# Weight remainders and mixer steps moved from GpSimd to VectorE in a two-block network on one core

## Chip, core and metric

The kernel runs on one core of a Trainium2 chip. The metric is the device time of one execution in microseconds (us), the median of three runs. A core has five engines that run side by side, each with its own queue that is worked off in order: TensorE (PE, with its weight loads shown as PEld), VectorE (DVE), ScalarE (ACT), GpSimd (POOL) and SyncE (SP), which here only issues loads. An instruction waits on semaphores at the head of its engine's queue; everything behind it on that engine waits too.

## What is computed

A sequence of 256 tokens of width 1024 goes through two different blocks, all in float32. The first has two layers of feed-forward, mixer, feed-forward; the second has a mixing stage (retention and dilated attention), a feed-forward and a gated embedding.

```
for layer in range(2):
    x = x + 0.5 * swiglu(rmsnorm(x, norm_ffn1[layer]), ffn1_gate, ffn1_up, ffn1_down)
    x = x + hybrid_mixer(rmsnorm(x, norm_mix[layer]), ...)      # three mixers side by side
    x = x + 0.5 * swiglu(rmsnorm(x, norm_ffn2[layer]), ffn2_gate, ffn2_up, ffn2_down)
x = rmsnorm(x, norm_final)
# second block
proj = rmsnorm_2(h, g_pre_mix) @ w_in_2
h = h + rmsnorm_2(mixed @ w_o_2, g_post_mix)       # mixed: retention and dilated attention, gated
h = h + rmsnorm_2(square(relu(rmsnorm_2(h, g_pre_mlp) @ w_up_2)) @ w_down_2, g_post_mlp)
h = h + rmsnorm_2(sigmoid(rmsnorm_2(h, g_pre_ple) @ w_ple_gate_2 + b) * (p @ w_ple_in_2), g_post_ple)
```

The hybrid mixer joins a gated delta rule (with a triangular solve over 128 tokens), a gated linear attention (scores by halving levels) and a gated linear recurrence.

## The kernel before

Weights stream from DRAM once, in 562 chunks of mostly 256 rows by 512 columns, loaded by SP into `raw` (four buffers). For accuracy each chunk is split into two tiles: `wh` is the chunk rounded by a ScalarE copy (L94), and `wl = raw - wh` is the remainder, one two-input subtraction (L97 on GpSimd, L99 on VectorE). `wh` and `wl` have three buffers each. A product then takes three matmuls for each weight tile and token tile: L146 to L148 where tokens are the output's rows (`gemm_tok`), L190 to L192 where features are (`gemm_feat`). The activations are split in the same way after a transpose on TensorE (`split`, L199 to L203).

Who computes a remainder is set by a string, `split_on`, read cyclically: "p" is GpSimd, "v" is VectorE. Outside the mixers it is "ppv", two of three on GpSimd. In a mixer each product has a string of its own in `MIX_ORDER`, which also is the order in which the mixer's steps are emitted: the recurrence's product `rg`, the small product `ba`, `k`, the decays (`gates`), the delta rule's keys and first solve (`dk`, `solve0`), the linear attention (`hg`, `vg`, `hgs`), and so on. `HG_POOL` says for each of the seven levels of `hgs` which engine computes the exponents (L900, L901) and the keys (L903). Four more steps of a mixer are fixed on GpSimd: the masks of the solve (L718, L719), the product of query and key (L871), and the gates of the recurrence (L988, L989, L995, L996).

The steps of VectorE in a mixer that the text names: the convolution of the recurrence (L964, L967) and of the delta rule (L628), the polynomial of a softplus (L383, L384), the predicated copies of the solve (L716), the queries of a level (L909). Every norm ends in a chain of tiny VectorE steps for x to the power -0.5 (L212 to L229).

The code is emitted in one order, and a scheduler then fixes each engine's queue ahead of the run, with priorities by that order and durations of its own. So a change of engine moves other instructions as well.

Of the kernel before, what the change touches and what calls it, by code (L numbers as in the profile page):

```python
# [19 lines left out]
# w ** -0.5 near 1 as a quadratic  # L20
# [3 lines left out]
class Weights:  # L24
    """All large weights as one array in DRAM, chunk after chunk in the order of use, each chunk
    with one contiguous run a partition. The host's side of it is laid out as chunks are taken."""
# [12 lines left out]
class Weight:  # L39
# [3 lines left out]
    def chunk(self, k0, nkt, c0, n):  # L43
        """Rows k0..k0+nkt*P, columns c0..c0+n as [P, nkt, n]."""
        a = self.all
        part = self.array[k0:k0 + nkt * P, c0:c0 + n].reshape(nkt, P, n).transpose(1, 0, 2)
        a.parts.append(part.reshape(-1))
        o, a.off = a.off, a.off + part.size
        return a.dram[o:a.off].rearrange("(p k c) -> p k c", p=P, k=nkt)


class Ctx:
    """Pools, constants and the pieces every sublayer uses."""

    def __init__(self, tc, stack):
# [15 lines left out]
        self.nw = 0  # L71
        self.nx = 0
        self.xtags = ("xa", "xb")   # two banks each; a phase may keep to one pair
        self.split_on = "ppv"   # who takes the remainders of the weight chunks: GpSimd or DVE
# [12 lines left out]
    def wchunk(self, w, k0, nkt, c0, n, room=None):  # L87
# [7 lines left out]
        self.nw += 1  # L95
        if self.split_on[self.nw % len(self.split_on)] == "p":
            nc.gpsimd.tensor_tensor(l, raw, h.bitcast(F32), op=ALU.subtract)  # L97
        else:
            nc.vector.tensor_tensor(l, raw, h.bitcast(F32), op=ALU.subtract)  # L99
# [14 lines left out]
    def hT_tile(self, j, dtype=None):  # L114
        """The j-th (h, l) pair of 8-k-tile slots."""
        return tuple(self.keep.tile([P, 8, S], F32R, tag=f"hT{i}{j}", name=self.nm("hT")) for i in "hl")

    def scratch(self, which):
        """A slot of a hidden-operand tile as 2048 plain floats a partition."""
# [6 lines left out]
    def gemm_tok(self, xs, w, kt0, nkt, c0, n, outs=None, first=True, last=True, wk0=0):  # L126
        """xs: (h, l) of [P, KT, S]; w: dram [K, N]; k-tiles kt0..kt0+nkt of xs, columns c0..c0+n."""
# [11 lines left out]
    def mm_tok(self, o, xs, kt0, m, t, wh, wl, a, z):  # L139
        """o += x[:, token tile t] @ w over m k-tiles from kt0, in three float32r products each."""  # L140
# [9 lines left out]
    def gemm_rows(self, xs, w, nkt, tail, js):  # L150
        """[P tok, 1024] for both token tiles as outs[ch][t]; the last tail weight chunks of each half
        are taken by token tile, so that tile 0 is ready before tile 1. js: hidden-operand slots that
        are free to hold them."""
# [52 lines left out]
    def rsqrt(self, out, x, shape, mul=None):  # L206
        """out = mul * x ** -0.5 for x > 0 (tiles of the given shape); mul: a number or a [P, 1] tile."""
# [24 lines left out]
class Stream:  # L232
    """The residual stream, token-major, and its transposed and weighted form for the next product."""
# [8 lines left out]
    def norm_T(self, wT, extra=None, by_tok=False):  # L242
        """(h, l): x * w transposed, split; r: [P, 2] rsqrt(mean(x^2) + eps)."""
# [45 lines left out]
def hidden_T(c, hT, hc, t, f0, n):  # L289
    """Transpose hc [P tok, n] into hT[:, f0/P.., t-th half], split."""  # L290
# [42 lines left out]
def consts_np():  # L333
    """Tables that depend on shapes alone: [P, n, P]."""
# [3 lines left out]
    out["triu"] = (t <= s) * 1.0            # [s', s]: s' <= s  # L338
    out["sufs"] = (t > s) * 1.0             # [s', s]: s' > s
    out["negm"] = np.where(t > s, -1e30, 0.0)   # [s, t]: s > t  # L340
    own = lambda a: np.stack([a[r, 32 * (r // 32):32 * (r // 32) + 32] for r in range(P)])   # diagonal 32-blocks
# [1171 lines left out]
```

## Time and profile before

| quantity | value |
|---|---|
| runs of the kernel | 1861.69 us median (1858.45, 1861.69, 1861.82) |
| the profiled execution, first to last instruction | 1858.6 us |
| TensorE busy | 1764.4 us, 95% |
| VectorE busy | 935.6 us, 50% |
| ScalarE busy | 896.4 us, 48% |
| GpSimd busy | 925.1 us, 50% |
| mean granted TensorE clock | 0.974 |

The first mixer lies at about 205 to 410 us and the second at about 786 to 1000 us; before, between and after them are the feed-forwards, and the second block begins at about 1180 us. In these tables "busy" of an engine is the time in which one of its instructions runs, also when that instruction is itself held up; so a long mean duration of a small operation is to be compared with the shortest one of its kind.

### The profile page before, as it was taken

To read this page: it belongs to the slowest core of one execution; us is meant where nothing else is said; L and a number is where in the kernel's file an instruction comes from. 1 tells how busy PE (TensorE), PEld (TensorE's weight loads), DVE (VectorE), ACT (ScalarE), POOL (GpSimd) and SP (SyncE) were. 2 spreads that over 40 slices of the span, in tenths; PEclk is the share of its full clock that TensorE was granted. 3 is DMA by queue.
4 is the path that set the end of the run, shared out by engine and by line. 5 is a ranking of instruction groups with operands and counts; after the bars stand their busy time and mean duration, and the time that the engine had idled before them with its cause. 6 is when DMAs were issued, how large, how long until landed. Compare 5 with 4: busy or idle time off the path is not lost.

```text
span 1858.6 us, 24550 instructions
## 1 busy us (share of the span) xinstructions
PE 1764.4 (95%) x9216; PEld 1488.6 (80%) x9216; DVE 935.6 (50%) x1744; ACT 896.4 (48%) x1364; POOL 925.1 (50%) x449
## 2 busy tenths in 40 slices
PE   8999988999999999987889999999999999999995
PEld 6888877978888788877878888788878888778884
DVE  5334599853333332299964333533556543643246
ACT  4445563444444444455345445455444544555453
POOL 4556455235555555544415556454433455555561
PEclk9999988899999999998989999999999999999998
DMA  6546432235555555532224545455333456545561
GB/s 221 181 159 206 162 111 74 87 102 181 182 193 182 181 182 181 182 137 91 69 100 169 177 163 205 153 184 173 127 134 114 158 176 209 181 164 181 182 227 45
DMA packets 91639, 292.13 MB, mean 157 GB/s; under 512 B 11008, under 2 KB 23808, under 8 KB 91520
## 3 DMA queue, kind: packets, MB, share of 16 engines
q1 hardware_dynamic: 91376, 290.45, 46.0%
q8 instruction: 72, 1.18, 0.3%
q14 instruction: 47, 0.39, 0.1%
q10 hardware_dynamic: 144, 0.11, 0.0%
HBM read 289.47 MB, written 1.05 MB: 156 GB/s over the span
## 4 chain that ended last, share of the span: by engine, by line
PE 72%; DVE 15%; issue 6%; POOL 3%; ACT 2%; DMA 1%; DVEq 0%; SPq 0%; POOLq 0%; ACTq 0%
PE mm L147 21%; PE mm L148 21%; PE mm L146 20%; POOL wl L97 3%; DVE cv L628 2%; PE htr L295 2%; PE mm L191 1%; PE mm L192 1%; PE mm L190 1%; DVE scr L909 1%; DMA raw<-in_weights 1%; DVE wl L99 1%; ACT wh L94 1%; DVE hS L716 1%; DVE rxc L967 1%
## 5 line engine op out<-in xcount | busy, mean ns | idle before, releaser
L97 POOL TENSOR_TENSOR wl<-raw,wh 128x1024 fp32r<-128x1024 f32 (+2 forms) x359 | 839.1, 2340 | 808.3 <-ACT wh L94 754.4
L94 ACT CAST wh<-raw 128x1024 fp32r<-128x1024 f32 (+2 forms) x544 | 549.5, 1011 | 600.7 <-PE mm L148 442.6
L147 PE MATMUL mm<-wl,xTh 128*128 128x512 f32 (+2 forms) x1336 | 509.0, 383 | 10.1 <-DVE wl L99 8.8
L148 PE MATMUL mm<-wh,xTl 128*128 128x512 f32 (+2 forms) x1336 | 503.9, 381 | 8.3 <-DVE xTl L203 8.3
L99 DVE TENSOR_TENSOR wl<-raw,wh 128x1024 fp32r<-128x1024 f32 (+2 forms) x185 | 236.4, 1278 | 488.3 <-ACT wh L94 487.9
L146 PE MATMUL mm<-wh,xTh 128*128 128x512 f32 (+2 forms) x1336 | 474.1, 385 | 1.4 <-ACT wh L94 0.9
L147 PEld LDWEIGHTS mm<-wl,xTh 128*128 128x128 f32 x1336 | 254.5, 190 | 58.6 <-DVE wl L99 9.3
L148 PEld LDWEIGHTS mm<-wh,xTl 128*128 128x128 f32 x1336 | 253.4, 190 | 59.5 <-DVE xTl L203 11.2
L146 PEld LDWEIGHTS mm<-wh,xTh 128*128 128x128 f32 x1336 | 250.7, 190 | 51.8 <-ACT xTh L202 3.2
L147 PE MATMUL mm<-wl,hT 128*128 128x512 f32 x608 | 243.3, 401 | 2.8 <-POOL wl L97 2.6
L148 PE MATMUL mm<-wh,hT 128*128 128x512 f32 x608 | 240.3, 396 | 0.0
L146 PE MATMUL mm<-wh,hT 128*128 128x512 f32 x608 | 219.1, 397 | 4.8 <-DVE scr L571 4.8
L190 PE MATMUL mm<-xTh,wh 128*128 128x256 f32 x448 | 130.7, 295 | 14.1 <-DVE xp L620 14.1
L146 PEld LDWEIGHTS mm<-wh,hT 128*128 128x128 f32 x608 | 115.3, 190 | 30.8 <-DVE scr L571 5.2
L147 PEld LDWEIGHTS mm<-wl,hT 128*128 128x128 f32 x608 | 115.8, 190 | 29.6 <-POOL wl L97 5.4
L148 PEld LDWEIGHTS mm<-wh,hT 128*128 128x128 f32 x608 | 116.1, 191 | 24.4 <-DVE hT L203 0.3
L191 PE MATMUL mm<-xTl,wh 128*128 128x256 f32 x448 | 131.9, 296 | 1.1 <-DVE xTl L203 1.1
L192 PE MATMUL mm<-xTh,wl 128*128 128x256 f32 x448 | 129.6, 294 | 0.0
L190 PEld LDWEIGHTS mm<-xTh,wh 128*128 128x128 f32 x448 | 88.5, 198 | 15.8 <-issue 15.5
L191 PEld LDWEIGHTS mm<-xTl,wh 128*128 128x128 f32 x448 | 89.0, 199 | 3.4 <-DVE xTl L203 1.9
L192 PEld LDWEIGHTS mm<-xTh,wl 128*128 128x128 f32 x448 | 87.6, 198 | 2.0 <-issue 1.2
L200 DVE TENSOR_TENSOR hT<-htr,hT 128x512 fp32r<-128x512 f32 (+1 forms) x76 | 49.9, 660 | 75.6 <-ACT hT L199 75.6
(444 smaller groups left out, 1857.6 us busy)
## 6 DMA issues: line engine op xcount, KB each, us to landing
raw<-in_weights SPq DMA_DIRECT2D x514, 512.0 KB, 3.3
raw<-in_weights SPq DMA_DIRECT2D x32, 256.0 KB, 3.1
raw<-in_weights SPq DMA_DIRECT2D x16, 260.0 KB, 3.0
x_res<-in_x SPq DMA_DIRECT2D x2, 512.0 KB, 4.4
rowp<-in_b_gate SPq DMA_DIRECT2D x2, 512.0 KB, 5.3
out<-pg SPq DMA_DIRECT2D x4, 256.0 KB, 2.0
tab<-in_tab SPq DMA_DIRECT2D x1, 900.5 KB, 6.0
ctab<-in_tab SPq DMA_DIRECT2D x1, 900.0 KB, 9.5
```

The lines of the kernel that those rows point to most:

```text
L94: nc.scalar.copy(h, raw)
L97: nc.gpsimd.tensor_tensor(l, raw, h.bitcast(F32), op=ALU.subtract)
L99: nc.vector.tensor_tensor(l, raw, h.bitcast(F32), op=ALU.subtract)
L146: nc.tensor.matmul(o, xh[:, kt, tok], wh[:, k], start=a and k == 0, stop=False)
L147: nc.tensor.matmul(o, xh[:, kt, tok], wl[:, k], start=False, stop=False)
L148: nc.tensor.matmul(o, xl[:, kt, tok], wh[:, k], start=False, stop=z and k == m - 1)
L190: nc.tensor.matmul(o, wh[:, k, cs], xh[:, kt], start=a, stop=False)
L191: nc.tensor.matmul(o, wh[:, k, cs], xl[:, kt], start=False, stop=False)
L192: nc.tensor.matmul(o, wl[:, k, cs], xh[:, kt], start=False, stop=z)
L200: nc.vector.tensor_tensor(l, src, h.bitcast(F32), op=ALU.subtract)
L295: nc.tensor.transpose(ps[:, b], hc[:, b * P:(b + 1) * P], c.ident)
L628: nc.vector.scalar_tensor_tensor(o[:, b], xp[:, b2, tap:tap + S], wc(tap), o[:, b], op0=ALU.mult, op1=ALU.add)
```

## The change

All `wl` subtractions go to VectorE, in every product. So do the solve's two masks, the query-key product, the exponents and keys of all levels, and the four steps of the recurrence. GpSimd keeps memsets and one-input copies. The strings that chose the engine go away; the order of emission stays. (The diff also drops comments, so line numbers of the kernel after are a little lower: L99 becomes L93, L967 becomes L955.)

```diff
-        self.nw += 1
-        if self.split_on[self.nw % len(self.split_on)] == "p":
-            nc.gpsimd.tensor_tensor(l, raw, h.bitcast(F32), op=ALU.subtract)
-        else:
-            nc.vector.tensor_tensor(l, raw, h.bitcast(F32), op=ALU.subtract)
+        nc.vector.tensor_tensor(l, raw, h.bitcast(F32), op=ALU.subtract)
...
-MIX_ORDER = "rg:pvvp ba:pvvp k:pvpp gates dk solve0 hg:vppv vg:pppv hgs v:ppvp solve1 hgo both dv1 q:ppvp dv0 dq core0 core1 z:ppvv dout out:pvvvppvp".split()
-HG_POOL = ("vvvppvp", "ppvppvv")
+MIX_ORDER = "rg ba k gates dk solve0 hg vg hgs v solve1 hgo both dv1 q dv0 dq core0 core1 z dout out".split()
...
-        nc.gpsimd.tensor_tensor(LT32, LT, h4(K["mt32"]), op=ALU.mult)
-        nc.gpsimd.tensor_tensor(LT, LT, h4(K["mt64"]), op=ALU.mult)
+        nc.vector.tensor_tensor(LT32, LT, h4(K["mt32"]), op=ALU.mult)
+        nc.vector.tensor_tensor(LT, LT, h4(K["mt64"]), op=ALU.mult)
...
-        nc.gpsimd.tensor_tensor(qk, q, k, op=ALU.mult)
+        nc.vector.tensor_tensor(qk, q, k, op=ALU.mult)
...
-            on = lambda i: nc.gpsimd if HG_POOL[i][lv] == "p" else nc.vector
-            on(0).tensor_tensor(Av[:, :, 1], cv[:, :, 1], ref, op=ALU.subtract)
-            on(0).tensor_tensor(Av[:, :, 0], ref, cv[:, :, 0], op=ALU.subtract)
+            nc.vector.tensor_tensor(Av[:, :, 1], cv[:, :, 1], ref, op=ALU.subtract)
+            nc.vector.tensor_tensor(Av[:, :, 0], ref, cv[:, :, 0], op=ALU.subtract)
...
-            on(1).tensor_tensor(B, A, k, op=ALU.mult)
+            nc.vector.tensor_tensor(B, A, k, op=ALU.mult)
...
-        nc.gpsimd.tensor_scalar(ti, ti, 1.0, 0.5, op0=ALU.add, op1=ALU.mult)
-        nc.gpsimd.tensor_tensor(ti, ti, xc, op=ALU.mult)
+        nc.vector.tensor_scalar(ti, ti, 1.0, 0.5, op0=ALU.add, op1=ALU.mult)
+        nc.vector.tensor_tensor(ti, ti, xc, op=ALU.mult)
...
-        nc.gpsimd.tensor_scalar(g2, g2, 0.044715, 1.0, op0=ALU.mult, op1=ALU.add)
-        nc.gpsimd.tensor_tensor(g2, g2, gx, op=ALU.mult)
+        nc.vector.tensor_scalar(g2, g2, 0.044715, 1.0, op0=ALU.mult, op1=ALU.add)
+        nc.vector.tensor_tensor(g2, g2, gx, op=ALU.mult)
```

The first place is VectorE's queue early in the first mixer, before the change: `rxc` is the recurrence's convolution, `ab` and `gx` belong to the decays, `wl` are remainders of weight chunks.

```order
L964 TENSOR_SCALAR rxc_1927<-rxp_1921,colp 128x256 x2
L99 TENSOR_TENSOR wl_2013<-raw_2010,wh_2012 128x2x260
L967 SCALAR_TENSOR_TENSOR rxc_1927<-rxp_1921,colp,rxc_1927 128x256 x6
L562 TENSOR_SCALAR ab_2046<-mm_1972,r_1763 128x8
L582 TENSOR_TENSOR gx_2206<-ab_2046,hrows 128x4
L99 TENSOR_TENSOR wl_2090<-raw_2087,wh_2089 128x1024
```

The same place on VectorE after the change (L952, L955 and L93 are L964, L967 and L99 of before):

```order
L952 TENSOR_SCALAR rxc_1927<-rxp_1921,colp 128x256 x2
L93 TENSOR_TENSOR wl_2013<-raw_2010,wh_2012 128x2x260
L955 SCALAR_TENSOR_TENSOR rxc_1927<-rxp_1921,colp,rxc_1927 128x256 x2
L93 TENSOR_TENSOR wl_2031<-raw_2028,wh_2030 128x2x260
L955 SCALAR_TENSOR_TENSOR rxc_1927<-rxp_1921,colp,rxc_1927 128x256 x2
L93 TENSOR_TENSOR wl_2060<-raw_2057,wh_2059 128x1024
L955 SCALAR_TENSOR_TENSOR rxc_1927<-rxp_1921,colp,rxc_1927 128x256 x2
L93 TENSOR_TENSOR wl_2090<-raw_2087,wh_2089 128x1024
L551 TENSOR_SCALAR ab_2046<-mm_1972,r_1763 128x8
```

Two remainders that GpSimd had (`wl_2031`, `wl_2060`) now stand between the six steps of the convolution.

The second place is VectorE's queue near the end of the program, in the norm after the second block's feed-forward, before the change; `rsy`, `rsw`, `rsa` and `pr` are the power -0.5, `x_res` is the residual stream.

```order
L220 SCALAR_TENSOR_TENSOR rsy_15354<-rsa_15356,rsy_15354 128x1
L222 TENSOR_SCALAR rsw_15355<-rsy_15354 128x1
L223 SCALAR_TENSOR_TENSOR rsa_15356<-rsy_15354,rsw_15355,pm_2884_15348 128x1
L228 TENSOR_SCALAR rsy_15354<-rsy_15354,rr_13917 128x1
L229 SCALAR_TENSOR_TENSOR pr_2885_15349<-rsa_15356,rsy_15354 128x1
L1358 SCALAR_TENSOR_TENSOR x_res<-pf_15340,pr_2885_15349,x_res 128x512
```

After the change (L214 is L220 of before, and so on; `hT` here is room for a remainder of the last product's weights):

```order
L214 SCALAR_TENSOR_TENSOR rsy_15354<-rsa_15356,rsy_15354 128x1
L93 TENSOR_TENSOR wl_15477<-raw_15474,wh_15476 128x1024
L216 TENSOR_SCALAR rsw_15355<-rsy_15354 128x1
L93 TENSOR_TENSOR hT_15497<-raw_15518,hT_15496 128x1024
L217 SCALAR_TENSOR_TENSOR rsa_15356<-rsy_15354,rsw_15355,pm_2884_15348 128x1
L197 SCALAR_TENSOR_TENSOR xTl_15369<-xtr_15371,colp,xTh_15368 128x128
L222 TENSOR_SCALAR rsy_15354<-rsy_15354,rr_13917 128x1
L223 SCALAR_TENSOR_TENSOR pr_2885_15349<-rsa_15356,rsy_15354 128x1
L1346 SCALAR_TENSOR_TENSOR x_res<-pf_15340,pr_2885_15349,x_res 128x512
```

Two remainders stand inside the chain here too.

## Rows read from the trace of the kernel before

**Rows 1.** The page: shares of the chain that ended last, by engine.
```profile
PE 72%; DVE 15%; issue 6%; POOL 3%; ACT 2%; DMA 1%; DVEq 0%; SPq 0%; POOLq 0%; ACTq 0%
```

**Rows 2.** Windows: stretch, length; busy PE, PEld, DVE, ACT, POOL; clock; DMA share, GB/s.
```profile
47.00:93.00 46.00, 46.00 (x211) 37.81 (x210) 14.61 (x17) 21.65 (x24) 26.16 (x11) 1.00 0.54 183
205.00:345.00 140.00, 118.95 (x842) 112.79 (x841) 129.80 (x220) 68.99 (x124) 65.38 (x48) 0.88 0.28 95
786.00:928.00 142.00, 118.24 (x891) 111.85 (x891) 132.97 (x235) 68.94 (x126) 66.43 (x49) 0.94 0.29 98
```

**Rows 3.** Timeline of GpSimd near the end: start us, duration us, instruction, idle before.
```profile
1814.17 2.38 POOL L97 TENSOR_TENSOR hT<-raw,hT 128x1024 fp32r<-128x1024 f32 x1 [3.23 <-PE xtr L262]
1816.50 2.35 POOL L97 TENSOR_TENSOR wl<-raw,wh 128x1024 fp32r<-128x1024 f32 x1
```

**Rows 4.** Timeline of VectorE over the same stretch.
```profile
1814.67 1.89 DVE L214 SCALAR_TENSOR_TENSOR rsw<-rsy,pm 128x1 f32<-128x1 f32 x1
...
1816.79 2.08 DVE L219 TENSOR_TENSOR rsa<-rsa,rsw 128x1 f32<-128x1 f32 x1
1818.89 2.26 DVE L220 SCALAR_TENSOR_TENSOR rsy<-rsa,rsy 128x1 f32<-128x1 f32 x1
1821.19 0.15 DVE L222 TENSOR_SCALAR rsw<-rsy 128x1 f32<-128x1 f32 x1
```

**Rows 5.** VectorE's groups at 205 to 345 us: busy us, mean ns | idle before.
```profile
L628 DVE SCALAR_TENSOR_TENSOR cv<-xp,colp,cv 128x256 f32<-128x256 f32 x24 | 17.6, 776 | 0.0
L909 DVE TENSOR_TENSOR scr<-hA,scr 64x256 f32<-64x256 f32 x14 | 12.1, 863 | 0.1
L99 DVE TENSOR_TENSOR wl<-raw,wh 128x1024 fp32r<-128x1024 f32 x8 | 9.8, 1221 | 11.2 <-ACT wh L94 11.1
L716 DVE COPY_PREDICATED hS<-ctab,LTm 32x128 f32<-32x128 int32 x8 | 9.0, 1125 | 0.1
L967 DVE SCALAR_TENSOR_TENSOR rxc<-rxp,colp,rxc 128x256 f32<-128x256 f32 x6 | 7.8, 1358 | 0.0
...
L900 DVE TENSOR_TENSOR hA<-scr 128x256 f32<-128x256 f32 x4 | 4.1, 1017 | 0.1
...
L901 DVE TENSOR_TENSOR hA<-scr 128x256 f32<-128x256 f32 x4 | 2.6, 638 | 0.0
...
L99 DVE TENSOR_TENSOR wl<-raw,wh 128x520 fp32r<-128x520 f32 x2 | 1.4, 696 | 0.6 <-ACT wh L94 0.6
```

**Rows 6.** VectorE lines over the whole run: shortest, median, longest ns.
```profile
L628 DVE SCALAR_TENSOR_TENSOR cv<-xp,colp,cv x72: 431/473/2622, 248.4 to 940.9; 128x256 f32<-128x256 f32 x72
...
L909 DVE TENSOR_TENSOR scr<-hA,scr x28: 388/587/1811, 298.3 to 909.1; 64x256 f32<-64x256 f32 x28
...
L716 DVE COPY_PREDICATED hS<-ctab,LTm x16: 250/1033/2364, 275.4 to 869.7; 32x128 f32<-32x128 int32 x16
...
L967 DVE SCALAR_TENSOR_TENSOR rxc<-rxp,colp,rxc x12: 469/1002/2621, 221.5 to 808.4; 128x256 f32<-128x256 f32 x12
...
L900 DVE TENSOR_TENSOR hA<-scr x8: 416/584/2480, 296.2 to 900.4; 128x256 f32<-128x256 f32 x8
```

**Rows 7.** GpSimd's groups at 205 to 345 us, first and last of twelve.
```profile
L97 POOL TENSOR_TENSOR wl<-raw,wh 128x1024 fp32r<-128x1024 f32 x15 | 37.0, 2471 | 36.5 <-ACT wh L94 25.1 <-PE hd L876 5.3 <-DVE rsw L217 3.5
...
L988 POOL TENSOR_SCALAR rth<-rth 128x512 f32<-128x512 f32 x1 | 0.6, 622 | 0.0
```

**Rows 8.** VectorE's first remainder in the first mixer, timeline.
```profile
204.44 1.22 DVE L99 TENSOR_TENSOR wl<-raw,wh 128x1024 fp32r<-128x1024 f32 x1 [9.80 <-ACT wh L94]
```

**Rows 9.** Timeline of VectorE at the start of the program.
```profile
9.58 2.29 DVE L384 TENSOR_SCALAR la<-la 128x4 f32<-128x4 f32 x1
...
14.59 2.31 DVE L229 SCALAR_TENSOR_TENSOR r<-rsa,rsy 128x2 f32<-128x2 f32 x1
```

**Rows 10.** Waits of the whole run: total us, times, longest us.
```profile
DVE hc L320 <- PE mm L148: 56.7, 20, 4.7
...
PEld mm L147 <- POOL wl L97: 7.8, 10, 2.0
```

More of the change, by code (lines that the diff above doesn't have):

```diff
@@ L70, in __init__ @@
         self.n = 0
-        self.nw = 0
         self.nx = 0
         self.xtags = ("xa", "xb")
-        self.split_on = "ppv"
         nc = self.nc
@@ L534, in __init__ @@
         for s in MIX_ORDER:
-            s, _, on = s.partition(":")
-            c.nw, c.split_on = -1, on or "pv"
             steps[s]()
@@ L539, in __init__ @@
                 c.xtags = ("xb",)
-        c.nw, c.split_on = -1, "ppv"
     def project(self, w_out):
```

## Prediction

> **What bounds the kernel now.** I read four views in turn. The chain of waits first: 72% of it is TensorE and 15% VectorE, only 3% GpSimd [rows 1], so the question is where VectorE's share lies. The busy times by stretch answer it. In a feed-forward TensorE is busy for 46.00 of 46.00 us at full clock, while VectorE has 14.61 us to do: nothing is to be won there by a faster VectorE. In the first mixer it is the reverse: VectorE is busy for 129.80 of 140 us, TensorE for 118.95 at a granted clock of 0.88; in the second it is 132.97 of 142 against 118.24 [rows 2]. So the mixers' first parts are VectorE's, about 282 us of the run, and TensorE's idle 21 and 24 us there are the most that a lighter VectorE can give back at the same clock.
>
> The timelines of both engines then show that much of this busy time isn't work. GpSimd's remainder that starts at 1814.17 ends at 1816.55; a VectorE step on one number per partition (L214) starts at 1814.67 and lasts 1.89 us, to 1816.56. The next remainder ends at 1818.85, and L219, begun at 1816.79, lasts 2.08 us, to 1818.87 [rows 3, 4]. When GpSimd is done, a step of the same size takes 0.15 us (L222) [rows 4]. So a VectorE instruction that meets a running GpSimd remainder is held to its end. The groups of the mixer show the same as means far above the shortest of their kind: 1358 ns against 469 for L967 [rows 5, 6]. The remainders that VectorE has itself all take about 1.22 us [rows 5].
>
> **What the change removes.** VectorE's holds in the first mixer, summed as (mean there less undisturbed) by count. For L628 I take the run's median as undisturbed, since most of its 72 are short; for the others, half of them held, the shortest [rows 5, 6]. L628: 24 x (776 - 473) = 7.3 us; L909: 14 x (863 - 388) = 6.7; L716: 8 x (1125 - 250) = 7.0; L967: 6 x (1358 - 469) = 5.3. Ten smaller lines, from L900, 4 x (1017 - 416) = 2.4, down to L901, 4 x (638 - 416) = 0.9, come to 17.7. Together 44.0 us. The same lines in the second mixer, counted in the same way, give 42.0.
>
> **What it adds.** Thirty-seven instructions of GpSimd in the first mixer, in twelve groups [rows 7]: 15 full remainders at VectorE's 1.22 = 18.3 us; 14 of half that size (three remainders, four keys, four masks, three products) at 0.70 = 9.8; six exponents at 0.42 = 2.5; two scalings of one operand, between 0.15 (the smallest step of all) and 0.70 each, taken at 0.42, since one whole operand is as much as the two halves of an exponent: 0.8 [rows 4 to 6]. That is 31.4 us in place of 44.0 (a remainder takes 2.47 us on GpSimd [rows 7]). The second mixer has one half remainder more: 32.1 for 42.0. Net: -12.6 and -9.9.
>
> **What else moves.** A remainder on VectorE waits at the head of its queue for ScalarE's `wh`, and the mixer's steps wait behind it; GpSimd took such waits at no cost (36.5 us before its 15) [rows 7]. The nearest price is that of VectorE's ten today: 11.2 + 0.6 us idle before them, of which 9.80 belong to the first alone, before the mixer starts [rows 5, 8]; the other nine cost 2.0, or 0.22 each. Eighteen more in the first mixer: 4.0; nineteen in the second: 4.2. The bounds are 0 (the order places a remainder late enough) and 1.18 each, the mean of all ten with the first (11.8 / 10), 44 in both. I take 0.22, because the new queue is like the old one: in the recurrence's convolution, which held four long-standing VectorE steps, the two added remainders stand with convolution steps between them. So the mixers give 12.6 - 4.0 = 8.6 and 9.9 - 4.2 = 5.7.
>
> At the ends of the program TensorE waits on VectorE too. In the first 17 us two steps are held, 2.29 and 2.31 us instead of some 0.16 [rows 9], 4.3 in all; the two remainders that held them come in their place at 1.22: -1.8 (between -4.3, if they fall outside the chain, and +2.4, if the holds were hidden). In the last norm three steps lose 1.89 + 2.08 + 2.26 - 3 x 0.15 = 5.8 us [rows 4] and three remainders come, 3.7: -2.1, with the bounds -5.8 and +3.7 by the same reasoning. The other norms I leave at nothing.
>
> In the feed-forwards the added 1.22 us per chunk is hidden by TensorE's own work: 211 matmuls in 46 us are 0.22 us each [rows 2], a full chunk has twelve (two row tiles, two token tiles, three terms), 2.6 us. Eleven GpSimd instructions there bring VectorE from 14.61 to 28 of 46 us. A remainder may now stand behind a VectorE step that waits for a product (L320: 56.7 us in 20 waits, 4.7 the longest [rows 10]); three buffers of `wl` leave up to two chunks, 5.2 us, in hand. I take 0; without that cover it is rival one. On the other side TensorE waited 7.8 us for GpSimd's remainders over the run [rows 10]: up to that is a further gain, which I don't count, since a remainder that is shorter may come later.
>
> One rule of the Trainium skill explains the holds: by "SBUF — State Buffer", section "Who interferes with whom", a VectorE instruction with two SBUF inputs and a GpSimd one that reads SBUF exclude each other for a whole instruction. The trace agrees, with L219 held for 2.08 us. A second rule speaks against the change: "Perfetto Trace Analysis", section "Optimizing Scalar/DVE Operations", says that with a saturated VectorE it may make sense to hand work to GpSimd, though it adds that this might not help since the two share a port. By the first half alone the time would be that of rival three.
>
> **Sum.** -8.6 - 5.7 - 1.8 - 2.1 = -18.2 us on a span of 1858.6: 1840.4. The runs lie between 1858.45 and 1861.82 around that span; with half of the 3.1 us to their median, 1842. The forecast's own range: 1824 (no waits at `wh`, a further 8.2, remainders outside the chain at both ends, 6.2, and half of the 7.8) to 1854 (half of the mixers' gain, 7, lost to TensorE's and ScalarE's chains, the waits at `wh` doubled, some 5 more).
>
> **Rivals.** First, slower: VectorE's queue now ties the feed-forwards together. The next block's remainders stand behind L320, which waits for TensorE, and TensorE then waits for the remainders. Against it stand the 5.2 us in hand and a VectorE at 28 of 46 us; for it, L320's waits, 2.8 us on average (56.7 / 20) [rows 10]. At one exposed remainder, 1.22 us, in each of 24 blocks (four feed-forwards of six) it costs 29: 1840.4 + 29.3, or 1871 as a median. It decides from 18.2 / 24 = 0.76 us a block.
>
> Second, the holds were hidden in the mixers: the solve's and the levels' round trips through TensorE and ScalarE set the pace, and VectorE's relief turns into idle time. TensorE's 118.95 of 140 busy [rows 2] speaks for it, VectorE's ten idle microseconds against. Only the ends gain: 1858.6 - 3.9 = 1854.7, 1856 as a median.
>
> Third, the relief isn't one: a step was long for a cause that stays (ScalarE's or TensorE's accesses), and the 31.4 and 32.1 us with their waits, 8.2, come on top of a full engine: 1858.6 + 71.7, about 1930. Ends that agree to 0.02 us [rows 3, 4] speak against it.
>
> That the change doesn't do what it says is ruled out by its order: GpSimd is left with memsets and one-input copies.
>
> **How the numbers follow.** Forecast 64%, first rival 15%, second 16%, third 5%. About 0.2%, 3.7 us, is what a measurement of this kernel can tell from no change. The forecast and most of the second rival are faster by more (1842 and 1856 against 1858.0): 0.64 + 0.09 = 0.73. The rest of the second rival is the same: 0.07. The first and third are slower: 0.20. The range reaches from 1816, a little below the forecast's own low end (the whole 7.8 and 4 us of a better clock), over the second rival to 1872, the first rival at its price; the waits at `wh` at their upper bound (44 in place of 8.2, or 1878), the third rival, the worse half of the first and the extreme low end are outside, less than 0.2.
>
> **What would show it right or wrong.** In the profile after, L967, L628 and L716 should fall to near 470, 470 and 300 ns in the mixers, L219 at the end to 0.15 us, and every remainder stand at 1.22. The first mixer's stretch should shrink by about 9 us and the second's by 6, with VectorE still busy for nine tenths of it, at some 117 us. The feed-forwards should stay at a TensorE busy throughout. The prediction is wrong if waits of TensorE for remainders, today 7.8 us for GpSimd's, grow to tens of microseconds, if VectorE's idle time before remainders in a mixer passes 10 us, or if the means of the mixer's steps stay above 0.7 us.

## The result: three times the gain that was forecast

| | before | after |
|---|---|---|
| median of four runs | 1861.2 us (1858.45 to 1861.82) | 1800.31 us (1800.02 to 1800.9) |
| profiled execution, first to last instruction | 1858.6 us | 1799.1 us |
| ratio after to before, 95% interval | | 0.9673 (0.9661 to 0.9686) |

The forecast was 1842 us with a range down to 1816. The way was right; the size, 18 us, was a third of the 61 us that came. The page of the kernel after, its line of busy times and its chain that ended last:

```profile
PE 1742.2 (97%) x9216; PEld 1477.1 (82%) x9216; DVE 1184.0 (66%) x2153; ACT 900.4 (50%) x1364; POOL 12.9 (1%) x40
...
PE 91%; DVE 4%; ACT 3%; issue 1%; DMA 1%; DVEq 0%; SPq 0%; ACTq 0%
```

VectorE's share of the chain fell from 15% to 4% [rows 1]. The more telling number is TensorE's busy time: the same 9216 matmuls took 1764.4 us before and 1742.2 now. So of the 59.5 us by which the profiled execution became shorter, 37.3 are less idleness of TensorE and 22.2 are matmuls that ran faster.

The places follow from matching the two executions matmul by matmul and cutting both at the same ones; where the order differs, a few fall on the other side of a cut (173 and 167 in the third stretch: eight small ones out, two large ones in, about equal in time). First the stretches before (length; busy PE, PEld, DVE, ACT, POOL; granted clock; DMA): the two mixers, the entry of the second block, and the stretch around the norm after its mixing stage:

```profile
203.00:412.00 209.00, 183.45 (x1242) 169.90 (x1241) 173.75 (x329) 102.82 (x191) 84.69 (x62) 0.90 0.29 97
780.00:1005.00 225.00, 194.36 (x1304) 176.64 (x1303) 181.01 (x344) 110.16 (x203) 92.69 (x63) 0.93 0.32 108
1172.00:1215.00 43.00, 38.89 (x173) 30.88 (x172) 27.30 (x69) 21.26 (x33) 20.79 (x8) 0.96 0.44 153
1590.00:1650.00 60.00, 56.88 (x247) 43.45 (x246) 39.11 (x78) 31.66 (x58) 30.45 (x13) 0.97 0.48 162
```

Then a steady feed-forward (as in [rows 2]) and the same four in the kernel after:

```profile
41.60:87.60 46.00, 46.00 (x211) 37.84 (x210) 27.65 (x29) 21.54 (x24) 0.00 (x0) 1.00 0.57 184
196.30:388.80 192.50, 176.80 (x1241) 164.80 (x1240) 162.83 (x376) 104.68 (x194) 5.55 (x17) 0.93 0.33 108
753.50:961.90 208.40, 189.68 (x1304) 175.10 (x1303) 171.86 (x393) 112.28 (x203) 3.57 (x13) 0.94 0.37 118
1128.30:1164.60 36.30, 36.30 (x167) 29.57 (x166) 29.05 (x78) 20.46 (x31) 0.00 (x0) 1.00 0.55 179
1539.80:1596.00 56.20, 54.99 (x246) 42.40 (x245) 43.32 (x90) 32.27 (x58) 0.00 (x0) 1.00 0.53 178
```

Each mixer gave 16.5 to 16.6 us, the entry of the second block 6.7, the stretch after its mixing stage 3.8. The start of the program gave 5.4, its end 5.2, the passage from the first layer's second feed-forward to the second layer's first 1.8, and everything between, some 1170 us of steady products, 3.5 together. A steady feed-forward took its 1.22 us per remainder without a trace, with VectorE at 27.65 us where the prediction had 28.

VectorE's groups in the first mixer after the change (L617, L897, L955 and L705 answer to L628, L909, L967 and L716 [rows 5]):

```profile
L93 DVE TENSOR_TENSOR wl<-raw,wh 128x1024 fp32r<-128x1024 f32 x34 | 41.3, 1219 | 10.4 <-ACT wh L92 10.4
...
L617 DVE SCALAR_TENSOR_TENSOR cv<-xp,colp,cv 128x256 f32<-128x256 f32 x36 | 15.5, 477 | 0.1
L897 DVE TENSOR_TENSOR scr<-hA,scr 64x256 f32<-64x256 f32 x14 | 5.8, 416 | 0.1
...
L955 DVE SCALAR_TENSOR_TENSOR rxc<-rxp,colp,rxc 128x256 f32<-128x256 f32 x6 | 2.6, 478 | 0.0
L705 DVE COPY_PREDICATED hS<-ctab,LTm 32x128 f32<-32x128 int32 x8 | 2.4, 295 | 0.1
```

The holds are gone: 1358 ns became 478, 1125 became 295, 776 became 477, and all remainders stand at 1.22. The same in the last norm (L208, L213 and L214 are L214, L219 and L220 [rows 4], which took 1.89 to 2.26 us):

```profile
1759.28 0.22 DVE L208 SCALAR_TENSOR_TENSOR rsw<-rsy,pm 128x1 f32<-128x1 f32 x1
...
1759.72 0.16 DVE L213 TENSOR_TENSOR rsa<-rsa,rsw 128x1 f32<-128x1 f32 x1
1759.92 0.16 DVE L214 SCALAR_TENSOR_TENSOR rsy<-rsa,rsy 128x1 f32<-128x1 f32 x1
```

So the mechanism of the prediction is there, with one limit: not every VectorE step that meets a running remainder is held, as the prediction put it. Between the two held steps of [rows 4] the kernel before has this one, which reads a single tile while GpSimd's remainder ran from 1816.50 to 1818.85 us [rows 3]:

```profile
1816.60 0.15 DVE L218 TENSOR_SCALAR rsa<-rsw 128x1 f32<-128x1 f32 x1
```

Another step with one tile to read, L384, was held for 2.29 us [rows 9], to 11.87 us, where a remainder of GpSimd ended at 11.84. What tells these two apart, no run here tests.

The experiments ask two things: is it the reading by GpSimd that holds VectorE, and where does the rest of the gain come from?

### The profile page after: what moved, and what is told of

Same layout as the page of the kernel before. It is cut to its first block, busy times and chain, and to the rows that moved or that the text cites. A ratio compares the mean times of both kernels' runs of the same rounds, so it can differ in the third digit from the quotient of the medians.

```text
span 1799.1 us, 24502 instructions
## 1 busy us (share of the span) xinstructions
PE 1742.2 (97%) x9216; PEld 1477.1 (82%) x9216; DVE 1184.0 (66%) x2153; ACT 900.4 (50%) x1364; POOL 12.9 (1%) x40
## 3 DMA queue, kind: packets, MB, share of 16 engines
HBM read 289.47 MB, written 1.05 MB: 161 GB/s over the span
## 4 chain that ended last, share of the span: by engine, by line
PE 91%; DVE 4%; ACT 3%; issue 1%; DMA 1%; DVEq 0%; SPq 0%; ACTq 0%
PE mm L140 24%; PE mm L141 24%; PE mm L142 24%; PE mm L186 3%; PE mm L184 3%; PE mm L185 3%; PE sv L698 2%; PE htr L289 2%; ACT wh L92 1%; DVE wl L93 1%; PE hS L902 1%; PE pv L1221 1%; PE dsc L1189 1%; DVE cv L617 1%; PE dsc L1188 0%
## 5 line engine op out<-in xcount | busy, mean ns | idle before, releaser
L93 DVE TENSOR_TENSOR wl<-raw,wh 128x1024 fp32r<-128x1024 f32 (+2 forms) x544 | 639.7, 1177 | 457.5 <-ACT wh L92 455.2
L140 PEld LDWEIGHTS mm<-wh,xTh 128*128 128x128 f32 x1336 | 247.0, 188 | 54.3 <-ACT xTh L196 7.4
L141 PEld LDWEIGHTS mm<-wl,hT 128*128 128x128 f32 x608 | 115.7, 190 | 24.4 <-DVE wl L93 0.9
L193 ACT CAST hT<-htr 128x512 fp32r<-128x512 f32 (+1 forms) x76 | 42.7, 563 | 64.9 <-PE htr L289 64.1
L194 DVE TENSOR_TENSOR hT<-htr,hT 128x512 fp32r<-128x512 f32 (+1 forms) x76 | 50.0, 660 | 30.6 <-ACT hT L193 30.6
```

The costliest lines, as they stand in the source:

```text
L140: nc.tensor.matmul(o, xh[:, kt, tok], wh[:, k], start=a and k == 0, stop=False)
L141: nc.tensor.matmul(o, xh[:, kt, tok], wl[:, k], start=False, stop=False)
L193: nc.scalar.copy(h, src)
L194: nc.vector.tensor_tensor(l, src, h.bitcast(F32), op=ALU.subtract)
```

## Experiments

All times below are medians; each was measured beside runs of the kernel before on the same chip (medians 1860.5 to 1862.4 us), and the ratio is to those. Some runs that add to the kernel after are written in the file of the kernel before, which still has `split_on`, so their line numbers are higher (L973 for L955).

**The two halves of the change.** First the remainders outside the mixers alone:

```diff
-        self.split_on = "ppv"
+        self.split_on = "v"
...
-        c.nw, c.split_on = -1, "ppv"
+        c.nw, c.split_on = -1, "v"
```

> The kernel before with one half of the change: outside the mixers every remainder is VectorE's, in the mixers all is as before. Theory of the holds, as the two traces now show it: the gain of the whole change lies 33.2 us in the mixers and 26.2 us outside, at the ends of the feed-forwards and blocks, so 1861 - 26 = 1835 us. The prediction's own sizes give it 3.9 us: 1857. If the stages hang together (an earlier start lost again in a mixer), 1845 or more.

Measured: 1833.96 us, 0.9859 (0.9839 to 0.9879), 26.5 us less. The prediction's 3.9 us for all ends was seven times too small. Stage by stage the gains are those of the whole change (5.5 at the start, 7.0 at the second block's entry, 6.0 at the end), and the mixers stay as they were (210.5 and 224.7 us).

Then the mixers alone: their strings all "v", `HG_POOL` all "v", the seven fixed steps on VectorE.

> The other half: in the mixers all remainders and steps are VectorE's, outside GpSimd keeps two remainders of three. Theory of the holds: 33.2 us less, 1828 us. The prediction's sizes (8.6 and 5.7 us): 1847. Together with the first half it should make up the whole, 59 to 61 us, if the parts don't depend on one another.

Measured: 1821.88 us, 0.9792 (0.9769 to 0.9815), 38.6 us less. The halves make up 65 us against 61 of the whole, nearly independent. In this run the mixers are 7.6 us shorter than in the whole change, at a higher granted clock (the table further down), and the norm behind the second block's mixing stage is 3.5 us longer than before; together that is about the odd 4 us; why the clock was higher wasn't taken apart.

**The mixers' half, cut once more.** Remainders of the mixers on VectorE, all other steps left on GpSimd (the strings of `MIX_ORDER` alone):

> The kernel before with the remainders of the mixers on VectorE (50 of them), while the mixers' other steps on GpSimd (masks, exponents, keys, gates) stay there and nothing is changed outside. Theory of the holds: the full remainders are the long reads, 2.4 us each, so most of the mixers' gain of 39 us comes with them: 1861 - 25 to 35, 1826 to 1836. Rival (by count of GpSimd's time: 41 of its 62 us in the first mixer's first part are remainders): two thirds, 1835. If VectorE's own queue paid for the remainders as the prediction said (1.22 + 0.22 each), and the holds by steps stay: about 1850.

Measured: 1836.50 us, 0.9869 (0.9853 to 0.9886), 24.4 us less. And the reverse, the steps on VectorE and all remainders as before:

> The kernel before with the mixers' steps on VectorE, all remainders as before. Theory of the holds: steps take 20 of GpSimd's 62 us in the first mixer's first part and their users lose less; 5 to 12 us of gain, 1849 to 1856. Rival (the remainders on GpSimd hold whatever VectorE does, and VectorE has 13 us more to do in a mixer where it was full): slower, up to 1880.

Measured: 1870.86 us, 1.0065 (1.0038 to 1.0092), 10 us *slower*. The parts give -24.4 and +10.0, their sum -14.4; together they give -38.6. The theory of the holds had 1826 to 1836 and 1849 to 1856: the first measurement lies just outside its range, next to the rival that went by GpSimd's time (1835), and the second is the other rival's, slower. With the remainders still on GpSimd, in the first mixer L967 stayed at 1359 ns, L909 and L716 fell only to 650 and 826, and of the moved steps the masks of L718 were held (1780 ns, 684 in the kernel after). So what the moved steps cost VectorE was about what its holds fell by. The mixers of the two kernels, first of the run with the remainders moved:

```profile
202.90:399.10 196.20, 180.84 (x1240) 167.83 (x1239) 161.91 (x353) 104.73 (x194) 35.41 (x38) 0.91 0.33 107
767.20:982.50 215.30, 192.99 (x1304) 176.78 (x1303) 172.78 (x368) 111.64 (x203) 41.65 (x39) 0.94 0.35 114
```

and of the run with the steps moved:

```profile
203.50:413.80 210.30, 182.38 (x1241) 168.38 (x1240) 175.52 (x348) 103.28 (x191) 65.81 (x43) 0.92 0.29 97
782.50:1010.30 227.80, 200.41 (x1304) 183.15 (x1303) 182.75 (x363) 110.85 (x203) 72.23 (x44) 0.92 0.32 106
```

VectorE's busy time fell by 12 and 8 us in the one, although it had 24 remainders more to do in each, and rose by 2 in the other.

**Is it the reading?** The kernel after, with work on GpSimd that nobody waits for. In the first of two kernels it reads `wh` with two inputs, in place of each remainder that GpSimd had:

```diff
+            q = n // 2
+            for a in range(nkt):
+                for b in range(2):
+                    x = h.bitcast(F32)[:, a, b * q:b * q + q]
+                    nc.gpsimd.tensor_tensor(self.junkp[:, :q], x, x, op=ALU.subtract)
```

> The kernel after, every engine's queue in the same order, but for each of the 371 chunks whose remainder GpSimd took before, GpSimd now also does four two-input steps of 128x256 that read the chunk's wh and write to a tile that nobody reads. No result of theirs is waited for; wh is released when they are done. Theory of the holds: VectorE is held again, for up to one such step at a time (some 0.6 us each, half of the old price), on top of its full work; the time goes back by 25 to 60 us, to 1825 to 1860. Rival (the gain came of remainders that are ready in 1.2 in place of 2.4 us, and of the new order): 1800, within 4.

In the second it fills the same tile instead, between two copies of two elements:

```diff
+            j = self.junkp[:, :n // 2]
+            nc.gpsimd.tensor_copy(j[:, 0:2], h.bitcast(F32)[:, 0, 0:2])
+            for _ in range(4 * nkt):
+                nc.gpsimd.memset(j, 0.0)
+            nc.gpsimd.tensor_copy(j[:, 0:2], h.bitcast(F32)[:, 0, 0:2])
```

> As the run with reads, but GpSimd's idle work is eight fills of 128x256 a chunk that read nothing, between two copies of two elements of wh that hold them in their place; about the same time on GpSimd. Theory of the holds by reading: VectorE isn't held, 1800 us within 4. If any work of GpSimd beside VectorE's costs (or the later release of wh), the time goes back as in the run with reads.

Measured: 1851.76 us with the reads, 1806.64 with the fills. GpSimd is busy for 1357 us in the one and 1251 in the other, VectorE for 1342.8 and 1186.7, against 1184.0 without either. Three of VectorE's groups in the first mixer, with reads:

```profile
L915 DVE TENSOR_TENSOR scr<-hA,scr 64x256 f32<-64x256 f32 x14 | 6.7, 480 | 0.1
...
L973 DVE SCALAR_TENSOR_TENSOR rxc<-rxp,colp,rxc 128x256 f32<-128x256 f32 x6 | 4.1, 725 | 0.0
L722 DVE COPY_PREDICATED hS<-ctab,LTm 32x128 f32<-32x128 int32 x8 | 3.2, 406 | 0.1
```

and with fills:

```profile
L915 DVE TENSOR_TENSOR scr<-hA,scr 64x256 f32<-64x256 f32 x14 | 5.8, 415 | 0.1
...
L973 DVE SCALAR_TENSOR_TENSOR rxc<-rxp,colp,rxc 128x256 f32<-128x256 f32 x6 | 2.6, 478 | 0.0
L722 DVE COPY_PREDICATED hS<-ctab,LTm 32x128 f32<-32x128 int32 x8 | 2.4, 294 | 0.1
```

With the reads, VectorE's 2153 steps and TensorE's 9216 matmuls stand in the order of the kernel after; with the fills, 19 and 40 of them are in other places. So 51 of the 61 us are undone by reads beside VectorE that give nobody a result, and fills of nearly the same length cost 6, two more than the 4 that were allowed for. The rival, that the gain came of earlier remainders or a better order, falls. What the 6 us are isn't settled: the small copies, which read too, or `wh` released later (VectorE was busy for only 2.7 us more). The Trainium skill, in "SBUF — State Buffer", section "Who interferes with whom", says that a VectorE instruction with two SBUF inputs contends with a GpSimd instruction that reads SBUF, not with one that only writes it; 725 ns against 478 agree.

**What a remainder costs VectorE now.** The kernel after, with remainders done twice over the same tile; first those that GpSimd had in the mixers. The trace has 48 of them, 24 in each, where the expectation counted 50.

```diff
             nc.vector.tensor_tensor(l, raw, h.bitcast(F32), op=ALU.subtract)
+            if self.split_on != "ppv":
+                nc.vector.tensor_tensor(l, raw, h.bitcast(F32), op=ALU.subtract)
```

> The kernel after with the 50 remainders of the mixers that were GpSimd's before done twice by VectorE, the second time over the same tile. The price of VectorE's time in the mixers as they now are. If VectorE still bounds them, as it did before: 50 x (1.22 less 0.08 of overlap) = 57 us, 1857. If TensorE's own work bounds them now (the chain of waits of the kernel after is nearly all TensorE there): less than half, 1802 to 1825.

Measured: 1850.50 us, 50.2 us more, 1.05 us for each of the 48. The chain of waits of the kernel after, nearly all TensorE, had suggested less than half of that: the theory that TensorE's own work bounds the mixers now falls. But the price isn't VectorE's time alone:

```profile
197.10:419.10 222.00, 193.08 (x1238) 178.78 (x1237) 184.17 (x394) 104.29 (x190) 6.43 (x17) 0.86 0.28 91
784.00:1014.90 230.90, 205.03 (x1304) 189.09 (x1303) 195.01 (x416) 111.64 (x202) 3.85 (x13) 0.87 0.31 105
```

TensorE's busy time grew by 16 and 15 us for the same matmuls, and the granted clock fell from 0.93 and 0.94 to 0.86 and 0.87.

Those outside the mixers, done twice; the trace has 323 of them, where the expectation counted 335:

> The kernel after with the 335 remainders outside the mixers that were GpSimd's before done twice by VectorE: 335 x 1.14 = 382 us of VectorE's time. The prediction took one such remainder each to be hidden under TensorE; if the cover has room for another (VectorE would be at some 85% in a feed-forward), only the ends of the stages pay: 1800 to 1815. If the in-order queue ties the column blocks together (the prediction's first rival): 1.22 us in each of 24 blocks or more, 1829 and up.

Measured: 1829.31 us, 29 more. Some 20 of them lie at the ends of stages and at the program's start and end (9 us at the end alone), the rest in feed-forwards, where VectorE is then busy for 83 to 86% of the time. One remainder per chunk is hidden there, a second not quite. The number lies on the bound of the second reading, that the queue ties the column blocks together; the ends, not the blocks, carry most of it.

**The middle of the feed-forwards back to GpSimd.** The remainders there, two of three in chunks 12 to 57; the trace has 120 on GpSimd, where the expectation counted 123:

```diff
+        on = nc.gpsimd if self.mid and 12 <= self.nw < 58 and self.nw % 3 else nc.vector
+        on.tensor_tensor(l, raw, h.bitcast(F32), op=ALU.subtract)
```

> The kernel after, but in the middle of each feed-forward (chunks 12 to 57 of about 70) two remainders of three are GpSimd's again, 123 in all; the ends of the feed-forwards, the mixers and the second block stay VectorE's. If the gain outside the mixers comes of the ends alone, as the stages of the two traces show it (the steady feed-forwards gave 0.5 to 1.3 us each): 1800 to 1804. If the holds cost all along a feed-forward: in proportion to the remainders, 26 x 123 / 335 = 10 us, 1810. If GpSimd's share frees VectorE for the mixers that follow (they were 3 and 4 us shorter in the run that changed the mixers alone): 1793.

Measured: 1799.98 us, the same as the kernel after, as the first reading had it. But two differences cancel in it: its four feed-forwards were 5 us longer in sum, about half of what the second reading gave the holds along them, and its mixers 3 and 4 us shorter. GpSimd's share need not be the reason for the shorter mixers: the next run has them too, without any such share. That outside the mixers the ends make the gain rests on the stages of the two traces; this run doesn't speak against it.

**What a gap costs TensorE.** One remainder in the middle of each feed-forward repeated, so that TensorE runs dry once:

```diff
+        for _ in range(1 + (self.rep if self.nw == 23 else 0)):
+            nc.vector.tensor_tensor(l, raw, h.bitcast(F32), op=ALU.subtract)
```

> The kernel after, with one remainder in the middle of each of the four feed-forwards (chunk 23) done 6, 8, 11 and 16 times more by VectorE over the same tile: 6.8, 9.1, 12.5 and 18.2 us in its queue. TensorE has some 5 us in hand and then stands still, for about 2, 4, 7 and 13 us. If a gap costs its own length alone: 26 us, 1826. If TensorE's clock falls behind a gap, as it stood at 0.55 for 3.7 us behind the 3.7 us of idleness at 1188 us of the kernel before: 1.7 us more for each gap, 1833, and the granted clock is below 1 right behind each.

Measured: 1843.59 us (a single run). The four gaps came to 3.8, 6.2, 9.3 and 16.4 us, each of them a wait of 1.55 us, a few matmuls and then the rest, and TensorE's idleness in the four feed-forwards grew by 38 in all, more than the 26 worked out. Its busy time there grew by 14 for the same matmuls; and the mixers of this run were 10 us shorter, at a clock of 0.95 and 0.96 and for a reason that isn't known, which makes up the 43. Both readings were too low; the sign of the second, a clock below 1 behind each gap, came. Windows in the third and fourth feed-forward: a stretch of the gap (in the third), then 3.6 us each behind it.

```profile
658.60:662.20 3.60, 0.03 (x1) 0.04 (x1) 3.44 (x3) 0.00 (x0) 0.00 (x0) 0.50 0.00 0
662.20:665.80 3.60, 3.60 (x9) 2.83 (x10) 0.00 (x0) 0.00 (x0) 0.00 (x0) 0.50 0.43 146
665.80:669.40 3.60, 3.60 (x16) 2.96 (x15) 1.62 (x2) 1.64 (x2) 0.00 (x0) 0.93 0.00 0
1052.70:1056.30 3.60, 3.59 (x9) 2.82 (x10) 0.00 (x0) 0.00 (x0) 0.00 (x0) 0.50 0.39 146
1056.30:1059.90 3.60, 3.60 (x12) 2.87 (x11) 1.40 (x2) 1.63 (x2) 0.00 (x0) 0.65 0.00 0
1059.90:1063.50 3.60, 3.60 (x20) 2.96 (x19) 3.25 (x5) 1.64 (x2) 0.00 (x0) 1.00 0.46 150
```

Behind the gap the clock stands at 0.50, its lower level of 1.2 GHz: 9 matmuls in 3.6 us, where at full clock there are 20. Over the third feed-forward TensorE was busy for 157.79 us where it was 154.10 in the kernel after, over the fourth 169.97 for 166.40: 3.7 and 3.6 us, after 9.3 us of idleness and after 16.4. In the first two it was 3.0 and 3.7 us, after 3.8 and 6.2: twice the 1.7 of the expectation, and nearly the same whatever the gap.

**Can VectorE's relief be carried on?** Six kinds of one-input steps of the mixers from VectorE to ScalarE, for example:

```diff
-        nc.vector.tensor_scalar(ti, ti, 1.0, 0.5, op0=ALU.add, op1=ALU.mult)
+        nc.scalar.activation(ti, ti, AF.Copy, scale=0.5, bias=0.5)
```

> The kernel after, with six kinds of one-input steps of the mixers (the recurrence's first convolution tap, its gate and two scalings, the copy of the decays, in the first layer the linear attention's keys) on ScalarE in place of VectorE: some 4 us of VectorE's time in each mixer. At the price that doubling the mixers' remainders showed (1.0 us for each 1.14 us of VectorE): 7 us less, 1793. If ScalarE's queue, with the casts in it, delays the remainders instead: 1800 to 1806.

Measured: 1813.67 us, 0.9746 (0.9713 to 0.9780), 13 us slower than the kernel after. Neither expectation held.

```profile
196.10:391.40 195.30, 184.09 (x1240) 172.31 (x1239) 158.58 (x366) 108.53 (x204) 5.58 (x17) 0.90 0.33 106
756.40:973.60 217.20, 202.42 (x1304) 186.92 (x1303) 168.30 (x385) 115.47 (x211) 3.94 (x13) 0.88 0.36 113
```

VectorE has 4 us less to do in each mixer, as meant, and TensorE is idle for 11.2 and 14.8 us where it was 15.7 and 18.7. Yet the mixers are 3 and 9 us longer: the same matmuls take 7 and 13 us more, at a clock of 0.90 and 0.88. No gap of TensorE in these mixers is longer than 2.6 us, where the kernel after has 5.0 and 4.9. Why the clock fell with less idleness and shorter gaps (the waits lie in other places, in the new order) wasn't taken apart.

**The wait filled.** In the kernel after, TensorE stands still for 5 us early in each mixer; the matmuls behind the gap come 0.21 us apart, those ahead of it 0.115 (timeline of TensorE: start, duration, instruction, idle before):

```profile
230.15 0.28 PE L186 MATMUL mm<-xTh,wl 128*128 128x256 f32 x1
235.47 0.55 PE L184 MATMUL mm<-xTh,wh 128*128 128x256 f32 x1 [5.05 <-DVE xp L609]
235.83 0.41 PE L185 MATMUL mm<-xTl,wh 128*128 128x256 f32 x1
236.04 0.41 PE L186 MATMUL mm<-xTh,wl 128*128 128x256 f32 x1
```

So matmuls without a use were put into the wait:

```diff
         ps = self.gemm(c0, 512)
+        if c0 == 1536:
+            f = c.x_tile("fill", tag="xb")
+            for i in range(44):
+                nc.tensor.matmul(f[:, :S], self.xs[0][:, 0, :P], self.xs[1][:, 0], start=True, stop=True)
```

> The kernel after, with 44 matmuls of 128x256 more in each mixer, over operands that are there anyway, into a bank that nobody reads: TensorE's queue has 37 of them at the point where it stood still for 5.05 us in the first mixer (230.4 to 235.5 us) and 4.86 us in the second, each behind a granted clock of 1 and followed by matmuls at 0.21 in place of 0.115 us. They take 37 x 0.115 = 4.3 us of the wait and 0.8 us before it. If the slow stretch behind a gap is what idle TensorE costs beside its idleness, it goes away: 3.4 us or more in each mixer, less the 0.8: 1793 to 1797, with the granted clock of 1 behind the place. If VectorE sets the mixers' time whatever TensorE's clock: 1800 to 1803.

Measured: 1795.14 us, 0.9655 (0.9627 to 0.9682). The windows of the gap and of what stands behind it, in the kernel after:

```profile
230.00:235.50 5.50, 0.45 (x5) 0.29 (x4) 4.70 (x10) 5.00 (x8) 0.00 (x0) 0.82 0.47 147
235.50:242.50 7.00, 7.00 (x41) 7.00 (x42) 7.00 (x21) 2.54 (x6) 0.00 (x0) 0.65 0.08 34
```

and with the filling:

```profile
230.00:236.00 6.00, 6.00 (x54) 6.00 (x52) 5.45 (x12) 5.96 (x10) 0.00 (x0) 1.00 0.50 175
236.00:243.00 7.00, 7.00 (x61) 7.00 (x62) 7.00 (x19) 3.48 (x6) 0.00 (x0) 1.00 0.25 77
```

The clock stays at 1.00 and 61 matmuls go through in the 7 us in which 41 did. It is the fastest kernel of this study, 5 us by the medians; the intervals of the two ratios still overlap, so the step beyond the kernel after is shown at the place, and only likely in the total. Its mixers are 2 and 4 us shorter than the kernel after's, about as much as in the two runs above that filled nothing (the mixers' half alone and the middle on GpSimd; the table below).

## Why the prediction was right in kind and wrong in size

**What bounds the kernel** was read rightly: VectorE in the mixers, TensorE elsewhere. The first rival, slower feed-forwards, didn't come. The second and third fell: the mixers did give, and the long steps did shorten.

**What the change removes and adds**, the largest terms, was right within 1.7 us. VectorE's busy time fell from 173.8 to 162.8 us in the whole first mixer and from 181.0 to 171.9 in the second, -10.9 and -9.2, where the sum had -12.6 and -9.9. That it came so near is partly luck: the sum counted what GpSimd had in the mixers' first parts, 18 and 19 remainders, and the whole mixers moved 24 each, with holds of their own.

**The waits at `wh`** failed as a term of the sum. They were to cost 4.0 and 4.2 us on top. What VectorE waited before remainders in the first mixer, before the change (us, times):

```profile
  ACT wh L94: 12.3, 6
```

and after it, with 42 remainders for 17:

```profile
  ACT wh L92: 11.7, 12
```

Most of the 9.8 us before the first of them [rows 8] lie ahead of the mixer, which starts at 203.0 us in these cuts. Within the stretch VectorE stood before remainders for 3.9 us before the change and 11.6 after it; in the second mixer for 15.3 and 18.0. That is 10.4 us more, near the 8.2 forecast. But they didn't lengthen the mixers, because VectorE's other idle time, nearly all of it waits for TensorE and ScalarE, fell from 31.4 to 18.0 us in the first and from 28.7 to 18.5 in the second. The sum held that constant: it added waits to a queue that already stood idle for some 30 us in each mixer. How much of the fall comes of faster matmuls, and how much of work that now fills a former wait, no run takes apart. (The prediction's own sign of being wrong, more than 10 us idle before remainders in a mixer, came too, with 11.7 and 19.0; it was no good sign, for the kernel before already had 12.3 and 18.2.)

**TensorE's clock** was held constant; the text says "at the same clock" and goes on. This was the largest omission in the mixers. TensorE's busy time there fell by 6.7 and 4.7 us for the same matmuls. The table splits each mixer's length into TensorE's idleness and its busy time; since the matmuls are the same, a difference in busy time is matmuls at another speed.

| first mixer, second mixer | length, us | clock | TensorE idle, us | TensorE busy, us |
|---|---|---|---|---|
| before | 209.0, 225.0 | 0.90, 0.93 | 25.6, 30.6 | 183.5, 194.4 |
| after | 192.5, 208.4 | 0.93, 0.94 | 15.7, 18.7 | 176.8, 189.7 |
| mixers' half alone | 189.1, 204.2 | 0.95, 0.96 | 14.4, 16.2 | 174.7, 188.1 |
| remainders twice | 222.0, 230.9 | 0.86, 0.87 | 28.9, 25.9 | 193.1, 205.0 |
| middle on GpSimd | 189.5, 204.5 | 0.95, 0.95 | 15.4, 16.2 | 174.1, 188.3 |
| steps on ScalarE | 195.3, 217.2 | 0.90, 0.88 | 11.2, 14.8 | 184.1, 202.4 |
| wait filled (44 matmuls more in each) | 190.1, 204.3 | 0.96, 0.96 | 11.5, 12.2 | 178.7, 192.1 |

By this the change took 9.9 and 11.9 us of idleness away, 21.8 in both, and the faster matmuls add 6.7 and 4.7. The 21.8 are close to the 22.5 that VectorE's work alone was forecast to give (12.6 + 9.9); mixer by mixer they aren't, so the near match is partly luck. The doubled remainders cost 13.2 and 7.2 us of idleness and 16.3 and 15.3 of slower matmuls. The steps on ScalarE even saved 4.5 and 3.9 of idleness, and slower matmuls took 7.3 and 12.7. A long stall that VectorE passes on to TensorE was paid twice in these runs, once as idleness and once in the matmuls behind it; that idleness alone tells the price is not shown, as the steps on ScalarE say.

**The ends** failed in two steps. "The two remainders that held them come in their place at 1.22" subtracted 2.4 and 3.7 us; measured were -5.4 at the start and -5.2 at the end, close to the holds alone, 4.3 and 5.8. At the end that is right in kind: of the 5.2 us, 4.9 are less idleness of TensorE, so the remainders cost next to nothing there; why, no run takes apart. At the start the nearness is luck: TensorE's idleness fell by 1.2 us only, and 4.2 are faster matmuls, 0.23 in place of 0.43 us apart (last section). The two windows of before, then the same of after:

```profile
0.00:47.00 47.00, 38.55 (x151) 30.34 (x152) 24.11 (x71) 23.20 (x37) 23.25 (x19) 1.00 0.61 218
1790.00:1858.60 68.60, 49.74 (x214) 40.12 (x212) 43.11 (x99) 29.49 (x61) 22.56 (x10) 0.87 0.32 114
0.00:41.61 41.61, 34.33 (x151) 27.41 (x152) 27.01 (x79) 22.80 (x37) 3.73 (x10) 1.00 0.72 246
1735.70:1799.12 63.42, 49.44 (x215) 39.48 (x213) 43.26 (x108) 29.70 (x60) 0.00 (x0) 0.90 0.33 112
```

And "the other norms I leave at nothing" left out 12 us. At the second block's entry the trace of before had the same pattern: steps held for 3.50 us (two, for 1.28), 2.29 (for 0.16) and, further on, 2.34 (for 0.21), 6.5 us in all. Behind the first two of these holds TensorE had this gap:

```profile
1188.00:1192.30 4.30, 0.65 (x2) 0.21 (x2) 4.16 (x10) 0.00 (x0) 0.65 (x1) 0.99 0.37 122
1192.30:1196.00 3.70, 3.63 (x9) 2.91 (x10) 3.46 (x14) 0.87 (x2) 0.00 (x0) 0.55 0.31 96
```

After the change TensorE is busy there for all of 36.3 us, at a clock of 1.00: 6.7 us less, 4.1 of idleness and 2.6 of slow matmuls. The timelines of the other ends, read like those of the two in the sum, would have shown it.

**The sum**, then: 14.3 us forecast in the mixers for 33.1, 3.9 at the ends for some 23, nothing in the steady stretches for 3.5. In the mixers the missing 19 us are the waits that were added and cost no length (8) and the clock (some 11); at the ends, those that were left out (12), the remainders that were charged at the program's end (3), and the faster matmuls at its start (4).

## What to carry to other kernels

Where two engines exclude each other, the gain isn't the sum of the moved parts: one part alone can cost (the steps, +10 us), another gain (the remainders, -24.4) and both together give more than their sum (-38.6), because what stays behind goes on holding. A wait that is added to a queue with other waits need not add to the time. In a stretch where TensorE waits on another engine, count a long wait that goes twice: its own length, and the slow matmuls behind it, whose price is read from the granted clock of the windows behind such gaps. And when a pattern is found at one end of a stage, walk all the ends of all stages with the same ruler before putting nothing for the rest.

## What the hardware showed that was not expected

- Behind a gap TensorE's clock stood at 0.50, and the price was nearly one number: 3.0, 3.7, 3.7 and 3.6 us more of busy time after 3.8, 6.2, 9.3 and 16.4 us of idleness. A wait of 5 us filled with useless matmuls kept the clock at 1.00.
- Less idleness in sum isn't a higher clock: with steps on ScalarE TensorE was idle for 4 us less in each mixer, and the clock was lower by 0.03 and 0.06.
- GpSimd's fills beside VectorE, 1251 us busy, cost 6 us; its reads, 1357 us busy, 51. Whether VectorE held GpSimd's reads in turn (936 ns in the mean for 128x256) wasn't measured by itself.
- In the first 21 us of the kernel before, matmuls of 128x512 came 0.43 us apart, though the windows print a clock of 1.00 there: the trace has no record of the clock before 21.5 us, and the view prints 1.00 where there is none. In the run with the mixers' half, whose records begin at 9.4 us, the matmuls are as slow and the clock reads its lower level:

```profile
13.00:23.00 10.00, 7.75 (x19) 5.59 (x18) 7.57 (x16) 2.89 (x6) 6.76 (x5) 0.50 0.54 156
```

After the change they came 0.23 apart from 11 us on. At the start of a program the matmuls' own distance is the better witness.
